# Starting the first weight before the last quarter of x, with two turned columns to a PSUM bank

## The chip, the cores and the metric

The kernel runs on one core of one Trainium2 chip. The metric is the device time of one execution in microseconds, as a median over runs. The engines that matter here are PE (TensorE: matrix products and transposes), ACT (ScalarE), DVE (VectorE), POOL (GpSimd) and SP, whose queue issues the loads.

## What is computed

A trunk of two layers on x (256 tokens x 1024), all in fp32. Each layer is a SwiGLU block, a mixer (windowed attention beside a convolution), a second SwiGLU block and a gated embedding:

```python
for i in range(DEPTH):
    h = x + 0.5 * swiglu(rms_norm(x, norm_ffn1[i]), w_ffn1_in[i], w_ffn1_out[i])
    u = rms_norm(h, norm_mix[i])
    ...
    h = h + (g_attn * y_attn + g_conv * y_conv) @ w_o[i]
    h = h + 0.5 * swiglu(rms_norm(h, norm_ffn2[i]), w_ffn2_in[i], w_ffn2_out[i])
    x = h + (p[i] @ w_pe_proj[i]) * jax.nn.sigmoid(rms_norm(h, norm_pe[i]) @ w_pe_gate[i])
```

Only the very beginning matters here: x is read, turned so that the 1024 features lie on partitions, scaled by the gain norm_ffn1, and multiplied with the first columns of w_ffn1_in. The division by the root mean square is applied after the product, so the squares of x are needed only later.

## The kernel before

**Split numbers.** Every fp32 operand of a product is split in a high part (rounded to fp32r) and a low part (the rest). A product takes three steps for each block of 128 features: high by high, high by low, low by high. A weight is a block of 1024 x 128: 8 feature blocks, so 24 steps of 128x256. ACT makes the high part of a weight (`w_hi`, line 108), DVE the low part (`w_lo`, line 109, source less high part).

**Loading and splitting weights.** `Weights` holds the order of all pieces. SP issues their loads (line 82) into five `raw` buffers, of which x takes one (`x_ld`, line 197, in four quarters of 256 columns). `prep_upto` splits them into seven pairs of buffers. `get` hands out the next weight and splits ahead (`LOOK`, less `rest`); `later` puts a function in front of a later `get`. The first four weights (`quick`) are loaded as pieces of 512 KB for themselves: 0 and 1 make the first pair of products (gate and up), 2 and 3 the second.

**The start.** The order of ACT and DVE at the start is written by hand (`manual_schedule`), and PE's transposes and fillers are kept in program order. In this document column k of x is the block of 128 features number k. For each k PE does fillers (`work`, line 190: products of a constant, whose only use is to keep PE busy), then two transposes (line 517, one for each half of the tokens) into the PSUM tile `xT[k]`. ACT makes the high part `x0h` (line 523) and DVE the low part `x0l` (line 524), both from PSUM. Later `keep_x` copies `xT[k]` to `x32` (line 505; ACT does k = 5 and 7, DVE the others), ACT squares it (lines 443 and 445), and POOL adds the squares (line 446). The squares have two buffers, so ACT's square waits for POOL's add two places back.

PSUM has eight banks of 512 fp32 values per partition: four tiles of one bank (`mm_tile`) and two of two banks (`at_tile`). Before, columns 2 to 5 have an `mm_tile` each; 0 and 6, and 1 and 7, share an `at_tile`, each column in a bank for itself.

After the turning PE does four fillers (`BRIDGE`) and then weight 0 in `by_pass` (line 351): all eight steps of high by high, then x's low part, then the weight's low part. From the second pair on, `mm3` (line 342) does the three steps of one feature block after the other, so it wants the weight's low part at its third step.

Of the kernel before, what the change touches and what calls it, by code (L numbers as in the profile page):

```python
# [9 lines left out]
F32 = mybir.dt.float32  # L10
F32R = mybir.dt.float32r
AF = mybir.ActivationFunctionType
# [3 lines left out]
P = 128  # L16
T = 256
# [19 lines left out]
BACKGROUND = 800  # L37
WEIGHTS_LAG = 100
ATTN = 7
WARM, WAIT, BRIDGE = 7, (0, 0, 1, 0, 2, 0, 2, 0), 4  # L40
W_BUFS = 7
ROW = 64
G0, G1, G2 = 24, 16, 8
# [3 lines left out]
class Weights:  # L47
# [4 lines left out]
    def __init__(self, tc, raw_pool, w_pool):  # L52
        self.tc, self.nc = tc, tc.nc
        self.raw_pool, self.w_pool = raw_pool, w_pool
        self.units, self.specs = [], []
        self.raw, self.ready, self.held, self.hooks = {}, {}, {}, []
        self.next_load = self.next_prep = self.next_get = 0
        self.behind = ()
        self.rest, self.pin, self.lag, self.parts = 0, None, 0, 1

    def unit(self, k, n, sources):
        self.units.append((k, n, sources))
# [13 lines left out]
    def load_upto(self, u):  # L76
        while self.next_load <= min(u, self.limit(), len(self.units) - 1):
            k, n, sources = self.units[self.next_load]
            t = self.raw_pool.tile([P, KD * 256], F32, name="raw", tag="raw")
            v = t[:, : k * n].rearrange("p (k n) -> p k n", n=n)  # L80
            for place, src in sources:
                self.nc.sync.dma_start(place(v), src)
            self.raw[self.next_load] = v
            self.next_load += 1

    def prep_upto(self, i):
        nc = self.nc
        while self.next_prep <= min(i, len(self.specs) - 1):
            k, n, pieces, as_is, place = self.specs[self.next_prep]
            for u, *_ in pieces:  # L90
                self.load_upto(u + RAW_BUFS - 2)
                if u >= self.next_load:
                    return
            if as_is:
                ((u, k0, s0, _, w),) = pieces
                self.ready[self.next_prep] = self.raw[u][:, k0 : k0 + k, s0 : s0 + w]
                self.next_prep += 1
                continue
# [4 lines left out]
            step = k // self.parts  # L103
            for a, (u, k0, s0, d0, w) in ((a, p) for a in range(0, k, step) for p in pieces):
                at = slice(a, a + step)
                src = self.raw[u][:, k0 + a : k0 + a + step, s0 : s0 + w]
                parts = (
                    nc.scalar.copy(out=hv[:, at, d0 : d0 + w], in_=src),  # L108
                    nc.vector.tensor_tensor(  # L109
                        out=lv[:, at, d0 : d0 + w],  # L110
                        in0=src,
                        in1=hv[:, at, d0 : d0 + w].bitcast(F32),
                        op=ALU.subtract,
                    ),
                )
# [40 lines left out]
def encoder_kernel(ctx: ExitStack, tc: tile.TileContext, a: dict, out: bass.AP):  # L156
# [18 lines left out]
    def mm_tile(name):  # L175
        return mmp.tile([P, 512], F32, name=name, tag="mm")
# [18 lines left out]
    for i in range(4):  # L195
# [31 lines left out]


    ws = Weights(tc, raw_pool, w_pool)

    def whole(v):
        return v

    def cols_unit(w, k, c0, n):
        return ws.unit(k, n, [(whole, w[: k * P, c0 : c0 + n].rearrange("(k p) n -> p k n", p=P))])

    def ffn_specs(w_in, w_out, quick=False):
        for j in range(KF // 2):
            if quick and j == 0:
                for c in range(2):  # L240
                    for c0 in (0, FF):
                        u = cols_unit(w_in, KD, c0 + c * P, P)
                        ws.spec(KD, P, [(u, 0, 0, 0, P)])
                continue
            ug = cols_unit(w_in, KD, j * 256, 256)
            uu = cols_unit(w_in, KD, FF + j * 256, 256)
            for c in range(2):
                ws.spec(KD, P, [(ug, 0, c * P, 0, P)])
                ws.spec(KD, P, [(uu, 0, c * P, 0, P)])
        for f in range(KD // 2):  # L250
            us = [
                ws.unit(n, 256, [(whole, w_out[k0 * P : (k0 + n) * P, f * 256 : (f + 1) * 256].rearrange("(k p) n -> p k n", p=P))])
                for k0, n in KGROUPS
            ]
            for c in range(2):
                for u, (_, n) in zip(us, KGROUPS):
                    ws.spec(n, P, [(u, 0, c * P, 0, P)])
# [85 lines left out]
                if pin:  # L343
                    tc.keep_in_program_order(mm)

    def by_pass(ps, w, x):

        (wh, wl), (xh, xl) = w, x
        for i, (wa, xa) in enumerate(((wh, xh), (wh, xl), (wl, xh))):
            for k in range(KD):  # L350
                nc.tensor.matmul(
                    ps, wa[:, k, :], xa[:, k, :], start=i == 0 and k == 0, stop=i == 2 and k == KD - 1
                )

    def pair(name, x, fresh, early=False):


        if early and fresh:
            ps = mm_tile(name)
            work(BRIDGE, ps)  # L360
            ps = ps.rearrange("p (c t) -> p c t", c=2)
            return ps, [lambda c=c: by_pass(ps[:, c, :], ws.get(), x) for c in range(2)]
        if not fresh:
            ps = mm_tile(name).rearrange("p (c t) -> p c t", c=2)
            return ps, [lambda c=c: mm3(ps[:, c, :], ws.get(), x) for c in range(2)]
# [12 lines left out]
        return ps, [lambda: start(0), end]  # L378
# [116 lines left out]


    x_first = x_cur = new_x("xa", "x0")
    stat = Stat()
    with tc.manual_schedule(engines={mybir.EngineType.Activation, mybir.EngineType.DVE}):
        n_par = place_params(rows_first, ("norm_ffn1",), 0, mm_tile)  # L500
        xT = {}

        def keep_x(k):
            copy = nc.scalar.copy if k in (5, 7) else nc.vector.tensor_copy
            copy(out=x32[:, k, :], in_=xT[k])


        shared = [at_tile("ps_xt") for _ in range(2)]
        for k in range(KD):
            if 2 <= k < 6:  # L510
                xT[k] = mm_tile("ps_xt")[:, :T]
            else:
                c0 = 0 if k < 2 else 512
                xT[k] = shared[k % 2][:, c0 : c0 + T]
            work(WAIT[k], xT[k])
            for t in range(2):
                turned = nc.tensor.transpose(
                    xT[k][:, t * P : (t + 1) * P], x_ld[:, t, k * P : (k + 1) * P], ident
                )
                tc.keep_in_program_order(turned)  # L520
            gain = pcol("norm_ffn1", 0, k)
            xh, xl = (x[:, k, :] for x in x_cur)
            nc.scalar.activation(out=xh, in_=xT[k], func=AF.Copy, scale=gain)
            nc.vector.scalar_tensor_tensor(
                out=xl, in0=xT[k], scalar=gain, in1=xh.bitcast(F32), op0=ALU.mult, op1=ALU.subtract
            )
# [742 lines left out]
```

## Time and profile before

| what | us |
|---|---|
| median of three runs | 1090.41 (1089.34 to 1090.47) |
| the profiled execution | 1088.88 |
| its span on the core | 1087.1 |
| PE's first step on weight 0 | 9.66 |
| PE's first step on weight 1 | 12.61 |
| PE's first step on weight 2 | 15.33 |
| SP's issues of x and the first nine pieces | 0.72 to 19.4 |

A row of the timeline has the start in us from the span's start, the duration from the first start to the last end, the engine, the line in the kernel before, the operation, the tile written and those read, and how many instructions it stands for; in brackets is how long the engine had been idle ahead of it, and what it waited for. Instructions overlap at their ends, so a row of two is shorter than twice one. A row of the groups has the line, engine, operation, shapes and count, then busy us and mean ns of one, then idle us ahead of them and what ended most of it. A row of waits has who waited for whom, the total in us, how often, and the longest.

### The profile page before, as it was taken

What the parts mean: (1) busy time and instruction counts of PE and PEld (TensorE: products, weight loads), DVE (VectorE), ACT (ScalarE), POOL (GpSimd) and SP (SyncE); (2) the same over time, 40 slices, a digit from 0 to 9 for tenths busy, and PEclk for the clock granted to TensorE, in tenths of its full rate; (3) what the DMA queues carried; (4) which work ended last, traced back from release to release, by engine and by line L of the source; (5) the groups of instructions that cost most, each with busy time, mean ns of one, the idle gap of its engine ahead of it and who ended that gap; (6) DMA issues with size and microseconds to landing.
All of it is one profiled execution on the core that took longest, in us unless ns stands there. A gap on an engine that the chain in (4) does not pass through costs nothing.

```text
span 1087.1 us, 22045 instructions
## 1 busy us (share of the span) xinstructions
PE 1079.0 (99%) x9182; PEld 1059.3 (97%) x9182; DVE 820.7 (75%) x1229; ACT 619.8 (57%) x1039; POOL 84.7 (8%) x123
## 2 busy tenths in 40 slices
PE   9999999999999999999999999999999999999998
PEld 8999999999899999999999999999998999999998
DVE  6877666799989777666887776659999987776664
ACT  7655445676767455445765554447776665554453
POOL 2000001220002000001110000113100100000110
PEclk9999999999999999999999999999999999999999
DMA  9876546556066646546556554576633666564531
GB/s 311 287 245 221 180 164 225 174 178 179 20 232 226 223 165 219 182 165 230 185 183 209 180 198 148 198 233 194 155 117 131 219 204 210 179 198 148 198 117 39
DMA packets 195439, 203.01 MB, mean 187 GB/s; under 512 B 3731, under 2 KB 188643, under 8 KB 195340
## 3 DMA queue, kind: packets, MB, share of 16 engines
q1 hardware_dynamic: 195308, 201.60, 56.2%
q8 instruction: 72, 1.18, 0.4%
q14 instruction: 27, 0.22, 0.1%
q10 hardware_dynamic: 32, 0.01, 0.0%
HBM read 200.53 MB, written 1.06 MB: 185 GB/s over the span
## 4 chain that ended last, share of the span: by engine, by line
PE 90%; DVE 5%; ACT 2%; issue 1%; DMA 1%; SPq 0%; POOL 0%; POOLq 0%
PE ps_gu L342 43%; PE ps_fo L342 22%; PE ps_c L342 4%; PE ps_wo L342 4%; PE ps_pe L342 4%; PE ps_ao L949 3%; PE ps_g L342 2%; DVE y L672 2%; PE ps_co L1053 2%; DVE w_lo L109 2%; PE ps_pp L342 1%; DVE s L838 1%; ACT s L846 1%; PE ps_q L780 1%; PE ps_q L782 1%
## 5 line engine op out<-in xcount | busy, mean ns | idle before, releaser
L109 DVE TENSOR_TENSOR w_lo<-raw,w_hi 128x1024 fp32r<-128x1024 f32 (+2 forms) x377 | 450.3, 1200 | 198.6 <-ACT w_hi L108 198.5
L108 ACT CAST w_hi<-raw 128x1024 fp32r<-128x1024 f32 (+2 forms) x377 | 387.8, 1035 | 361.2 <-PE ps_gu L342 191.6
L342 PE MATMUL ps_fo<-h_hi,w_lo 128*128 128x256 f32 x704 | 193.0, 275 | 0.0
L342 PE MATMUL ps_fo<-h_lo,w_hi 128*128 128x256 f32 x704 | 193.0, 275 | 0.0
L342 PE MATMUL ps_fo<-h_hi,w_hi 128*128 128x256 f32 x704 | 193.0, 275 | 0.0
L342 PEld LDWEIGHTS ps_fo<-h_lo,w_hi 128*128 128x128 f32 x704 | 131.8, 188 | 0.0
L342 PEld LDWEIGHTS ps_fo<-h_hi,w_hi 128*128 128x128 f32 x704 | 131.8, 188 | 0.0
L342 PEld LDWEIGHTS ps_fo<-h_hi,w_lo 128*128 128x128 f32 x704 | 131.8, 188 | 0.0
L446 POOL TENSOR_TENSOR sq_acc<-sq_acc,sq 128x256 f32<-128x256 f32 x56 | 52.6, 938 | 827.7 <-ACT sq L445 827.4
L672 DVE SCALAR_TENSOR_TENSOR y<-cpad,cw,y 128x256 f32<-128x256 f32 x240 | 100.9, 471 | 0.1
L342 PE MATMUL ps_gu<-xf1l,w_hi 128*128 128x256 f32 x352 | 97.1, 276 | 0.0
L342 PE MATMUL ps_gu<-xf0l,w_hi 128*128 128x256 f32 x352 | 97.1, 276 | 0.0
L342 PE MATMUL ps_gu<-xn0h,w_hi 128*128 128x256 f32 x352 | 97.0, 276 | 0.0
L342 PE MATMUL ps_gu<-xf1h,w_hi 128*128 128x256 f32 x352 | 97.0, 275 | 0.0
L342 PE MATMUL ps_gu<-xf0h,w_hi 128*128 128x256 f32 x352 | 97.0, 275 | 0.0
L342 PE MATMUL ps_gu<-xf0h,w_lo 128*128 128x256 f32 x352 | 96.9, 275 | 0.0
L342 PE MATMUL ps_gu<-xf1h,w_lo 128*128 128x256 f32 x352 | 96.9, 275 | 0.0
L342 PE MATMUL ps_gu<-xn0h,w_lo 128*128 128x256 f32 x352 | 96.8, 275 | 0.0
L342 PE MATMUL ps_gu<-xn0l,w_hi 128*128 128x256 f32 x352 | 96.8, 275 | 0.0
L342 PE MATMUL ps_gu<-x0h,w_lo 128*128 128x256 f32 x336 | 92.8, 276 | 0.3 <-DVE w_lo L109 0.3
L342 PE MATMUL ps_gu<-x0h,w_hi 128*128 128x256 f32 x336 | 92.9, 276 | 0.0
L342 PE MATMUL ps_gu<-x0l,w_hi 128*128 128x256 f32 x336 | 92.5, 275 | 0.0
(260 smaller groups left out, 2683.4 us busy)
## 6 DMA issues: line engine op xcount, KB each, us to landing
raw<-in_w_ffn_in_dram SPq DMA_DIRECT2D x86, 1024.0 KB
raw<-in_w_in_dram SPq DMA_DIRECT2D x30, 1024.0 KB
raw<-in_w_ffn_out_dram SPq DMA_DIRECT2D x32, 896.0 KB
raw<-in_w_ffn_out_dram SPq DMA_DIRECT2D x16, 1024.0 KB
raw<-in_w_o_dram SPq DMA_DIRECT2D x8, 1024.0 KB
raw<-in_w_pe_gate_dram SPq DMA_DIRECT2D x8, 1024.0 KB
raw<-in_w_attn_out_dram SPq DMA_DIRECT2D x8, 512.0 KB
raw<-in_w_conv_out_dram SPq DMA_DIRECT2D x4, 1024.0 KB
```

What stands on the lines that cost most here:

```text
L108: nc.scalar.copy(out=hv[:, at, d0 : d0 + w], in_=src),
L109: nc.vector.tensor_tensor(out=lv[:, at, d0 : d0 + w], in0=src, in1=hv[:, at, d0 : d0 + w].bitcast(F32), op=ALU.subtract,),
L342: mm = nc.tensor.matmul(ps, wa[:, k0 + k, cols], xa[:, kx, :], start=a, stop=b)
L446: nc.gpsimd.tensor_tensor(out=self.acc, in0=self.acc, in1=sq, op=ALU.add)
L672: last_tap[0] = nc.vector.scalar_tensor_tensor(out=y[:, i, :], in0=src, scalar=w, in1=y[:, i, :], op0=ALU.mult, op1=ALU.add)
L780: nc.tensor.matmul(o_, u[0][:, kx, ts], wh[:, k, :], start=kx == 0, stop=False)
L782: nc.tensor.matmul(o_, u[1][:, kx, ts], wh[:, k, :], start=False, stop=kx == KD - 1)
L838: nc.vector.tensor_tensor_reduce(out=s[:, c, :], in0=ps[:, c, :], in1=bias[:, v * GROUP + c, off : off + T], scale=1.0, scalar=sink[:, hd ...
L846: nc.scalar.activation(out=s[:, c, :], in_=s[:, c, :], func=AF.Exp, bias=nm[:, c : c + 1], accum_out=den[:, c : c + 1],)
L949: nc.tensor.matmul(ps[:, c * T : (c + 1) * T], w[:, k, c * P : (c + 1) * P], x[:, k, :], start=k == 0, stop=k == KC - 1,)
L1053: mm = nc.tensor.matmul(ps[:, c, :], wa[:, k, c * P : (c + 1) * P], ya[:, k, :], start=(i, k) == (0, 0), stop=(i, k) == (2, KC - 1),)
```

## The change

1. The first piece of weights is loaded in two transfers, feature blocks 0 to 5 (`CUT` = 6) ahead of x's last quarter and blocks 6 and 7 behind it; the second piece in two halves. Their splits are cut at the same places.
2. PE turns columns 0 to 5, then does the high by high steps of weight 0 on blocks 0 to 5 (`by_pass` with an order and with `last=False`), and only then turns columns 6 and 7. The remaining 18 steps follow: low by high and high by low on 0 to 5, then all three on 6 and 7. The first pair's products have a two-bank tile (`first_ps`).
3. The eight turned columns lie in four one-bank tiles, columns 2i and 2i + 1 in the two halves of tile i.
4. All copies to `x32` come after the splits of weights 0 and 1, in order of k. The splits of weights 2 and 3 stand ahead of the squares number 2 and 4 (counted from 0; 2 and 5 before). `get` is called once ahead of the rest, so weights 4 and on are queued one `get` later than before, and the product of the squares' sum (`ps_stat`) too.
5. One warm-up filler fewer (`WARM` 6), and other fillers between the columns.

```diff
-WARM, WAIT, BRIDGE = 7, (0, 0, 1, 0, 2, 0, 2, 0), 4
+WARM, WAIT, BRIDGE = 6, (0, 0, 2, 0, 1, 0, 0, 0), 4
+CUT = 6
...
             for i, (place, src) in enumerate(sources):
                 self.nc.sync.dma_start(place(v), src)
+                if (self.next_load, i) == (0, 0):
+                    self.between()
...
+    for i in range(3):
+        load_x(i)
...
+    ws.between = lambda: load_x(3)
...
-                        u = cols_unit(w_in, KD, c0 + c * P, P)
+                        u = cols_unit(w_in, KD, c0 + c * P, P, (() if c else (KC,) if c0 else (CUT,)))
...
         if early and fresh:
-            ps = mm_tile(name)
-            work(BRIDGE, ps)
-            ps = ps.rearrange("p (c t) -> p c t", c=2)
-            return ps, [lambda c=c: by_pass(ps[:, c, :], ws.get(), x) for c in range(2)]
+            order = [(i, 0, KD) for i in range(3)]
+            return first_ps, [lambda: None, lambda: by_pass(first_ps[:, 1, :], ws.get(), x, order)]
...
+    first_ps = at_tile("ps_gu").rearrange("p (c t) -> p c t", c=2)[:, :, :T]
...
-        shared = [at_tile("ps_xt") for _ in range(2)]
-        for k in range(KD):
-            if 2 <= k < 6:
-                xT[k] = mm_tile("ps_xt")[:, :T]
-            else:
-                c0 = 0 if k < 2 else 512
-                xT[k] = shared[k % 2][:, c0 : c0 + T]
+        banks = [mm_tile("ps_xt") for _ in range(KD // 2)]
+
+        def turn_x(k):
+            xT[k] = banks[k // 2][:, k % 2 * T : (k % 2 + 1) * T]
             work(WAIT[k], xT[k])
...
-            if k == 3:
-                keep_x(2)
-                keep_x(3)
-        ws.parts = 2
-        ws.prep_upto(0)
-        ws.parts = 1
+        for k in range(CUT):
+            turn_x(k)
+            first_part(k)
+            second_part(k)
+        splits = []
+        ws.cuts = (CUT,)
+        ws.prep_upto(0, splits)
+        w_first = ws.ready[0]
+        work(BRIDGE, first_ps[:, 0, :])
+        high, low, high_end, low_end = splits
+        high()
+        low()
+        by_pass(first_ps[:, 0, :], w_first, x_cur, ((0, 0, CUT),), last=False)
+        high_end()
+        for k in range(CUT, KD):
+            turn_x(k)
+            first_part(k)
+            second_part(k)
+        low_end()
+        order = ((1, 0, CUT), (2, 0, CUT), (0, CUT, KD), (1, CUT, KD), (2, CUT, KD))
+        by_pass(first_ps[:, 0, :], w_first, x_cur, order, first=False)
+        ws.cuts = (KC,)
         ws.prep_upto(1)
-        for k in (4, 5, 6, 7, 0, 1):
+        ws.cuts = ()
+        order = range(KD)
+        for k in order:
             keep_x(k)
-        for i, k in enumerate((2, 3, 5, 4, 6, 7, 0, 1)):
-            if i in (2, 5):
-                ws.prep_upto(2 + i // 5)
+        for i, k in enumerate(order):
+            if i in (2, 4):
+                ws.prep_upto(1 + i // 2)
             squared = stat.add(x32[:, k, :])
+    ws.rest = LOOK
+    ws.get()
+    ws.rest = 0
```

Where instructions move, the built programs are shown as they stand, an engine's rows in order, with the semaphores that an instruction waits for in brackets: `DMAHW` counts transfers, and the others count the finished instructions of the engine they name.

PE from the first transposes to weight 0, in the program before (line 517 turns a column, line 190 is a filler, line 351 a step):

```order
L517 MATMUL ps_xt<-ident,x_ld 128x128 [waits DMAHW1_49]
L517 MATMUL ps_xt<-ident,x_ld 128x128 x3
L190 MATMUL ps_xt<-ones_d 128x128
L517 MATMUL ps_xt<-ident,x_ld 128x128 [waits DMAHW2_49]
L517 MATMUL ps_xt<-ident,x_ld 128x128 x3
L190 MATMUL ps_xt<-ones_d 128x128 [waits PE_49]
L190 MATMUL ps_xt<-ones_d 128x128
L517 MATMUL ps_xt<-ident,x_ld 128x128 [waits DMAHW3_49]
```

And in the program after, in the same place (lines 530, 195 and 367):

```order
L530 MATMUL ps_xt<-ident,x_ld 128x128 [waits DMAHW1_49]
L530 MATMUL ps_xt<-ident,x_ld 128x128
L530 MATMUL ps_xt<-ident,x_ld 128x128 [waits DVE_49]
L530 MATMUL ps_xt<-ident,x_ld 128x128
L195 MATMUL ps_xt<-ones_d 128x128 x2
L530 MATMUL ps_xt<-ident,x_ld 128x128 [waits DMAHW2_49]
...
L367 MATMUL ps_gu<-x0h,w_hi 128x256 [waits Activation_49]
L367 MATMUL ps_gu<-x0h,w_hi 128x256 x5
L530 MATMUL ps_xt<-ident,x_ld 128x128 [waits DMAHW5_49]
L530 MATMUL ps_xt<-ident,x_ld 128x128
L530 MATMUL ps_xt<-ident,x_ld 128x128 [waits DVE_49]
L530 MATMUL ps_xt<-ident,x_ld 128x128
```

Two columns followed each other on PE with no wait between them; now the second column of each bank stands behind a wait on DVE, and the last bank's two columns stand between the first six steps of weight 0 and the others.

ACT from the split of weight 1 to that of weight 3, in the program before (line 108 casts a weight, 505 copies a column, 443 and 445 square):

```order
L108 CAST w_hi<-raw 128x1024 [waits DMAHW6_49]
L505 COPY x_117<-ps_xt 128x256 [waits DVE_49] x2
L443 ACTIVATE sq_acc<-x_117 128x256
L445 ACTIVATE sq<-x_117 128x256
L108 CAST w_hi<-raw 128x1024 [waits DMAHW7_49]
L445 ACTIVATE sq<-x_117 128x256 [waits Activation_49]
L445 ACTIVATE sq<-x_117 128x256 [waits DVE_49,Pool_49] x2
L108 CAST w_hi<-raw 128x1024 [waits DMAHW0_49]
```

And in the program after (lines 112, 521, 458 and 460):

```order
L112 CAST w_hi<-raw 128x512 [waits DMAHW7_49]
L112 CAST w_hi<-raw 128x512 [waits DMAHW0_49]
L521 COPY x_115<-ps_xt 128x256 [waits DVE_49] x2
L458 ACTIVATE sq_acc<-x_115 128x256
L460 ACTIVATE sq<-x_115 128x256
L112 CAST w_hi<-raw 128x1024 [waits DMAHW1_49]
L460 ACTIVATE sq<-x_115 128x256
L460 ACTIVATE sq<-x_115 128x256 [waits Pool_49]
L112 CAST w_hi<-raw 128x1024 [waits DMAHW2_49]
```

Both programs have the two copies ahead of the cast of weight 2. Before, they waited for the low parts of columns 5 and 7 on DVE; now the columns share banks with 4 and 6, and the copies wait for DVE's copies of those, which stand fifth and sixth in DVE's row:

```order
L539 SCALAR_TENSOR_TENSOR x0l<-ps_xt,par,x0h 128x256 [waits Activation_49] x6
L113 TENSOR_TENSOR w_lo<-raw,w_hi 128x768 [waits DMAHW4_49,Activation_49]
L539 SCALAR_TENSOR_TENSOR x0l<-ps_xt,par,x0h 128x256 [waits Activation_49] x2
L113 TENSOR_TENSOR w_lo<-raw,w_hi 128x256 [waits DMAHW6_49]
L113 TENSOR_TENSOR w_lo<-raw,w_hi 128x512 [waits DMAHW7_49,Activation_49]
L113 TENSOR_TENSOR w_lo<-raw,w_hi 128x512 [waits DMAHW0_49,Activation_49]
L521 COPY x_115<-ps_xt 128x256 x6
L113 TENSOR_TENSOR w_lo<-raw,w_hi 128x1024 [waits DMAHW1_49,Activation_49]
```

DVE did two of its copies among the low parts of x and four ahead of weight 2's low part; now all six stand ahead of that.

More of the change, by code (lines that the diff above doesn't have):

```diff
@@ L58, in __init__ @@
         self.behind = ()
-        self.rest, self.pin, self.lag, self.parts = 0, None, 0, 1
+        self.rest, self.pin, self.lag, self.cuts = 0, None, 0, ()
     def unit(self, k, n, sources):
@@ L80, in load_upto, with prep_upto @@
             v = t[:, : k * n].rearrange("p (k n) -> p k n", n=n)
-            for place, src in sources:
+            for i, (place, src) in enumerate(sources):
                 self.nc.sync.dma_start(place(v), src)
+                if (self.next_load, i) == (0, 0):
+                    self.between()
             self.raw[self.next_load] = v
             self.next_load += 1
-    def prep_upto(self, i):
+    def prep_upto(self, i, calls=None):
         nc = self.nc
@@ L102, in prep_upto @@
             lv = lo[:, place : place + k * n].rearrange("p (k n) -> p k n", n=n)
[L103 to L113, printed above, removed]
-                    ),
-                )
+            ends = (0, *self.cuts, k)
+            for (a, b), (u, k0, s0, d0, w) in ((ab, p) for ab in zip(ends, ends[1:]) for p in pieces):
+                hs, ls = hv[:, a:b, d0 : d0 + w], lv[:, a:b, d0 : d0 + w]
+                src = self.raw[u][:, k0 + a : k0 + b, s0 : s0 + w]
+                made = (
+                    lambda hs=hs, src=src: nc.scalar.copy(out=hs, in_=src),
+                    lambda hs=hs, ls=ls, src=src: nc.vector.tensor_tensor(
+                        out=ls, in0=src, in1=hs.bitcast(F32), op=ALU.subtract
+                    ),
+                )
+                if calls is not None:
+                    calls.extend(made)
+                    continue
+                parts = [call() for call in made]
                 if self.pin:
@@ L194, in encoder_kernel, with load_x @@
     xv = a["x"][0].rearrange("(t p) d -> p t d", p=P)
-    for i in range(4):
+    def load_x(i):
         s = slice(i * 256, (i + 1) * 256)
         nc.sync.dma_start(x_ld[:, :, s], xv[:, :, s])
+    for i in range(3):
+        load_x(i)
     col = {}
@@ L229, in encoder_kernel, with cols_unit @@
     ws = Weights(tc, raw_pool, w_pool)
+    ws.between = lambda: load_x(3)
     def whole(v):
         return v
-    def cols_unit(w, k, c0, n):
-        return ws.unit(k, n, [(whole, w[: k * P, c0 : c0 + n].rearrange("(k p) n -> p k n", p=P))])
+    def cols_unit(w, k, c0, n, cuts=()):
+        src = w[: k * P, c0 : c0 + n].rearrange("(k p) n -> p k n", p=P)
+        ends = (0, *cuts, k)
+        return ws.unit(k, n, [
+            (whole if not cuts else lambda v, a=a, b=b: v[:, a:b], src[:, a:b]) for a, b in zip(ends, ends[1:])
+        ])
     def ffn_specs(w_in, w_out, quick=False):
@@ L344, in mm3, with by_pass @@
                     tc.keep_in_program_order(mm)
-    def by_pass(ps, w, x):
+    def by_pass(ps, w, x, order, first=True, last=True):
         (wh, wl), (xh, xl) = w, x
-        for i, (wa, xa) in enumerate(((wh, xh), (wh, xl), (wl, xh))):
-            for k in range(KD):
-                nc.tensor.matmul(
-                    ps, wa[:, k, :], xa[:, k, :], start=i == 0 and k == 0, stop=i == 2 and k == KD - 1
-                )
+        passes = ((wh, xh), (wh, xl), (wl, xh))
+        steps = [(i, k) for i, k0, k1 in order for k in range(k0, k1)]
+        for n, (i, k) in enumerate(steps):
+            wa, xa = passes[i]
+            mm = nc.tensor.matmul(
+                ps, wa[:, k, :], xa[:, k, :], start=first and n == 0, stop=last and n == len(steps) - 1
+            )
+            tc.keep_in_program_order(mm)
     def pair(name, x, fresh, early=False):
         if early and fresh:
-            ps = mm_tile(name)
-            work(BRIDGE, ps)
-            ps = ps.rearrange("p (c t) -> p c t", c=2)
-            return ps, [lambda c=c: by_pass(ps[:, c, :], ws.get(), x) for c in range(2)]
+            order = [(i, 0, KD) for i in range(3)]
+            return first_ps, [lambda: None, lambda: by_pass(first_ps[:, 1, :], ws.get(), x, order)]
         if not fresh:
@@ L505, in keep_x @@
             copy(out=x32[:, k, :], in_=xT[k])
-        shared = [at_tile("ps_xt") for _ in range(2)]
-        for k in range(KD):
-            if 2 <= k < 6:
-                xT[k] = mm_tile("ps_xt")[:, :T]
-            else:
-                c0 = 0 if k < 2 else 512
-                xT[k] = shared[k % 2][:, c0 : c0 + T]
+        banks = [mm_tile("ps_xt") for _ in range(KD // 2)]
+        def turn_x(k):
+            xT[k] = banks[k // 2][:, k % 2 * T : (k % 2 + 1) * T]
             work(WAIT[k], xT[k])
```

9 lines of the change are left out of this document (5 added, 4 removed).

## Prediction

> **What bounds the kernel now.** I read the page first, then the waits of PE (TensorE), then the first 23 us of the timeline engine by engine, since the diff touches nothing later.
>
> The page's first part gives busy time, share of the span and instructions; the rows of PE's waits give the total, the number and the longest, in us.
>
> ```profile
> span 1087.1 us, 22045 instructions
> PE 1079.0 (99%) x9182; PEld 1059.3 (97%) x9182; DVE 820.7 (75%) x1229; ACT 619.8 (57%) x1039; POOL 84.7 (8%) x123
> ...
> PE ps_pt L865 <- ACT s L857: 1.5, 2, 0.7
> ...
> PE ps_gu L351 <- ACT w_hi L108: 0.6, 1, 0.6
> PE ps_gu L342 <- DVE w_lo L109: 0.3, 1, 0.3
> PE ps_xt L517 <- DMA x_ld<-in_x_dram: 0.2, 1, 0.2
> ```
>
> PE is busy from its first weight to the end and waits hardly anywhere. So the time is: when PE begins on the first weight, plus its steps, plus its stalls. A microsecond lost or won at the front is kept to the end. The front on PE (start, duration, operation, count; fillers and 128x128 fp32 products show two rows each):
>
> ```profile
> 1.12 3.36 PE L190 MATMUL ps_warm<-ones_d 128*128 128x128 f32 x14 [1.12 <-POOL ones_d L183]
> ...
> 4.62 0.66 PE L517 MATMUL ps_xt<-ident,x_ld 128*128 128x128 f32 x4
> ...
> 5.77 0.61 PE L190 MATMUL ps_xt<-ones_d 128*128 128x128 f32 x4
> 6.22 0.60 PE L517 MATMUL ps_xt<-ident,x_ld 128*128 128x128 f32 x4
> ...
> 7.51 0.66 PE L517 MATMUL ps_xt<-ident,x_ld 128*128 128x128 f32 x4 [0.24 <-DMA x_ld<-in_x_dram]
> ...
> 9.66 1.26 PE L351 MATMUL ps_gu<-x0h,w_hi 128*128 128x256 f32 x8 [0.60 <-ACT w_hi L108]
> ...
> 12.61 1.07 PE L351 MATMUL ps_gu<-x0h,w_hi 128*128 128x256 f32 x8
> 13.52 1.07 PE L351 MATMUL ps_gu<-x0l,w_hi 128*128 128x256 f32 x8
> ...
> 15.33 0.28 PE L342 MATMUL ps_gu<-x0h,w_hi 128*128 128x256 f32 x1
> ...
> 15.56 0.28 PE L342 MATMUL ps_gu<-x0h,w_lo 128*128 128x256 f32 x1
> ...
> 18.16 0.28 PE L342 MATMUL ps_gu<-x0l,w_hi 128*128 128x256 f32 x1
> 18.70 0.39 PE L342 MATMUL ps_gu<-x0h,w_lo 128*128 128x256 f32 x1 [0.26 <-DVE w_lo L109]
> ...
> 22.03 0.37 PE L342 MATMUL ps_gu<-x0h,w_lo 128*128 128x256 f32 x1
> ```
>
> PE begins at 9.66 when ACT's cast of the first weight is done, ends that weight at 12.61, the second at 15.33, and stalls at 18.70 for the low half of weight 3. Eight steps take 13.52 - 12.61 = 0.91, so 0.114 each. Beside it ACT, DVE and POOL:
>
> ```profile
> 5.16 0.47 ACT L523 ACTIVATE x0h<-ps_xt,par 128x256 fp32r<-128x256 f32 x1 [0.27 <-PE ps_xt L517]
> 5.53 0.83 ACT L523 ACTIVATE x0h<-ps_xt,par 128x256 fp32r<-128x256 f32 x2
> 5.67 0.48 DVE L524 SCALAR_TENSOR_TENSOR x0l<-ps_xt,par,x0h 128x256 fp32r<-128x256 f32 x1 [5.67 <-ACT x0h L523]
> 7.98 0.47 ACT L523 ACTIVATE x0h<-ps_xt,par 128x256 fp32r<-128x256 f32 x1 [0.51 <-PE ps_xt L517]
> 8.98 1.14 ACT L108 CAST w_hi<-raw 128x512 fp32r<-128x512 f32 x2 [0.17 <-DMA raw<-in_w_ffn_in_dram]
> 9.64 1.29 DVE L109 TENSOR_TENSOR w_lo<-raw,w_hi 128x512 fp32r<-128x512 f32 x2
> 11.50 0.64 ACT L505 COPY x<-ps_xt 128x256 f32<-128x256 f32 x2
> 12.77 1.41 DVE L505 COPY x<-ps_xt 128x256 f32<-128x256 f32 x4
> 13.60 0.73 ACT L445 ACTIVATE sq<-x 128x256 f32<-128x256 f32 x2
> 17.34 1.30 DVE L109 TENSOR_TENSOR w_lo<-raw,w_hi 128x1024 fp32r<-128x1024 f32 x1 [2.02 <-ACT w_hi L108]
> L108 ACT CAST w_hi<-raw 128x1024 fp32r<-128x1024 f32 x12 | 11.9, 1048 | 0.4 <-DMA raw<-in_w_ffn_in_dram 0.4
> L108 ACT CAST w_hi<-raw 128x512 fp32r<-128x512 f32 x2 | 1.1, 616 | 0.2 <-DMA raw<-in_w_ffn_in_dram 0.2
> L446 POOL TENSOR_TENSOR sq_acc<-sq_acc,sq 128x256 f32<-128x256 f32 x7 | 6.9, 991 | 12.1 <-ACT sq L445 11.8
> L109 DVE TENSOR_TENSOR w_lo<-raw,w_hi 128x1024 fp32r<-128x1024 f32 x10 | 11.9, 1224 | 4.7 <-ACT w_hi L108 4.7
> ```
>
> The turned columns go through a pipeline: ACT starts on column 1 at 5.53, before DVE starts on column 0 at 5.67. That overlap is possible because each column has its own tile.
>
> **The shared banks (the largest term).** In the changed program columns 2i and 2i+1 lie in one bank, and the order with its waits shows what follows: the second column's transposes wait on DVE, whose first work of all is column 0's low half. So PE turns column 1 only after ACT and DVE have read column 0. The link, from the rows: transposes to ACT 0.47 (7.51 to 7.98), ACT to DVE 0.51 (5.16 to 5.67), DVE 0.48, and 0.06 back to PE (17.34 + 1.30 to 18.70): 1.52 us between two columns that stood 0.23 apart. Two transposes take 0.23 (half of 6.22 less 5.77), and so does one filler.
>
> The first column starts at 4.4: its landing isn't shown, but it is at or before 4.62, and one warm-up filler fewer frees 0.48 (two rows of 3.36 / 14), so the bounds are 4.1 and 4.6. Then, column by column: 0 at 4.4, 1 at 5.92, two transposes and two fillers, 2 at 6.61, 3 at 8.13, two transposes and one filler, 4 at 8.59, 5 at 10.11. ACT starts on column 5 at 10.58 and is free 0.37 later (5.53 less 5.16), at 10.95. The cast of 6/8 of the first weight (128x768, no row) lies between 0.62 and 1.05; I take 0.83. PE begins at 11.84 with 0.06 for the signal. Before: 9.66. **Term 1: +2.2.**
>
> The early transfer, which is what the change is about, gains nothing here: x's quarters and 3/4 of the piece have landed long before 10.95 (the whole 512 KB piece had at 8.98), and even x's last quarter comes before its turn.
>
> **The first weight.** PE runs six steps (0.68), at 12.52 turns column 6, and column 7 stands next in its queue: it waits until 14.04, and the eighteen other steps of this weight, which need neither, wait behind it. They end at 14.04 + 0.23 + 18 x 0.114 = 16.32; the weight took 9.66 to 12.61, 2.95, and now 4.48. **Term 2: +1.5** (0.45 are the four transposes, which lay ahead of the weight before).
>
> **Weight 2's low half.** The second weight ends at 16.32 + 2.72 = 19.04; PE wants weight 2's low half at 19.27. DVE has, from column 7's low half at 14.04 + 0.98 = 15.02: that (0.39 step), the 128x256 rest (about 0.35, under half of the 128x512), two halves of 512 (1.29), at 17.0 six copies where four stood, 0.35 each by 1.41 / 4: the fifth and sixth end at 18.8 and 19.1. ACT's copies of columns 5 and 7 now share banks with these, and wait for them; ACT's queue holds behind them two squares and cast 2. So: copy 7 from 19.1 (0.32), two squares (0.73) to 20.1, cast 1.05 to 21.2, low half 1.22 to 22.45, PE at 22.5. Before: 15.56, with no wait. **Term 3: 22.5 - 19.27 = +3.2.** Check: 22.5 - 15.56 = 6.9 = 2.2 + 1.5 + 3.2.
>
> **Weights 3 and 4.** Weight 3's cast now follows two squares instead of standing behind a third that waits for POOL; its low half is ready near 24, and PE wants it at 25.2. The stall of before goes: 18.16 + 0.114 = 18.27 to 18.70. **Term 4: -0.4.** Weight 4's cast stands behind all squares, as before, and POOL's adds (0.99 each) pace them: the last square starts when five adds after 20.1 are through, 25.2 to 26.6 by mean pace or by the pace of before. So its low half lands at 27.8 to 29.2, wanted at 22.5 + 48 x 0.114 = 28.0. The step of before at 22.03 had the statistics product (0.25) ahead of it, which moves 24 steps later. **Term 5: +0.2, from -0.3 to +0.9.**
>
> The rest is cover: two more issues on SP, cuts of w1 in halves, ten casts ahead of the square root instead of seven (ACT is 1.05 per cast against 2.72 per weight of PE, so it runs ahead), one more DVE and ACT instruction. They cost nothing while weights are ready seven deep; if evacuations came late, PE would wait for a bank at the fifth pair, about 11 us after weight 4 starts, and the root is done about 10 us after cast 4 starts, which itself starts 2.3 us ahead. That is close, so up to +0.5 goes into the range.
>
> Sum: 2.2 + 1.5 + 3.2 - 0.4 + 0.2 = **+6.7 us**. The profiled execution took 1088.88 (span 1087.1 and 1.8 around it); it becomes 1095.6. The median of the three runs shown, 1090.41, lies 1.5 above that execution, so the median I predict is **1097.1**.
>
> **Where the skill speaks.** Row: ACT's 5.53 and DVE's 5.67 overlap, in two tiles. The Trainium skill, PSUM — Partial Sum Buffer, section "PSUM bank collisions raise a hardware error", says that two engines may not be in one bank (on the same partitions) at once, at any address, and that the compiler orders them. By that rule the turning is serial as above, +6.7; by the row alone, it would be the third rival's +0.3. The order's waits side with the rule; no trace here has a shared bank.
>
> **Rivals.**
> 1. *The array falls back to half rate.* The first fillers ran at 3.36 / 14 = 0.24 a row, later ones at about 0.11 (0.45 for four): PE starts slow and becomes fast with use. Between 4.4 and 11.8 it now works only 12 transposes and 7 fillers, 1.4 + 1.6 = 3.0 us of 7.4, and waits 3.2 later. Half rate through the turning adds some 0.1 per transpose pair and 0.23 per filler on the path, and 0.7 in the first six steps: +1.5; half rate in weight 2 adds 24 x 0.1 = 2.4. Against: no single idle stretch is over 2 us up to the first weight. Time: 1097.1 + 1.5 to 2.4, so 1098.6 to 1099.5. Chance 0.14. The Trainium skill, TensorE: Matmul & The Clock Gate, Part 1, has the fall need an idle window of about 3.4 us; by that rule this rival would not happen, and no run here shows such a gap.
> 2. *Only the turning is serial; ACT's copies don't hold the squares.* Then cast 2 starts after two squares that follow the second DVE copy (17.7), about 18.5, DVE is free at 19.1, and the low half is there at 20.35: term 3 becomes 1.1, the sum +4.6, the time 1095.0. Against: the order shows the wait on both copies. Chance 0.07.
> 3. *Not slower: the waits are met before PE arrives* and the turning overlaps as before. PE then starts when 3/4 of the piece has landed: x's end at 7.51 plus 128 KB more, at the 512 KB per 1.5 us from 7.5 to 8.98, is 7.9; with the cast 8.8. That is -0.9, the four transposes +0.45, DVE's two further copies and the squares ahead of cast 2 make weight 2 late by some 1.2 (its low half near T + 7.35 = 16.15 against 15.56 before), the stall -0.4, weight 4 +0.1: +0.3, 1090.7. It decides at one place: whether column 1's transposes start 0.2 or 1.5 us after column 0's. Against: no filler fills 1.3 us there. Chance 0.06. Even with weight 2's wait gone this gives -0.9, so faster by more than 0.2% (2.2 us) would need PE to begin at 7.5, before its operand.
>
> **Numbers.** Forecast 0.73, rivals 0.14, 0.07 and 0.06. The forecast's own range comes from the start of column 0 (0.4), the 768 cast (0.2 either way), term 5 (-0.5 to +0.7), late evacuations (0.5) and the spread of the three runs (1089.34 to 1090.47): 1095.4 to 1098.8. With most of rival 1 and the edge of rival 2 the range is 1094.8 to 1099.6. A difference of 0.2%, 2.2 us, is about what a measurement of this kernel can tell from no change; only rival 3 stays within it: same 0.06, faster 0.01, slower 0.93.
>
> **What would show it.** Right: in the timeline, second transposes of each bank 1.5 us behind the first, with PE waiting for DVE x0l; PE's first product of x0h and w_hi near 11.8; a wait of about 1.3 inside the first weight; a wait of 3 us for w_hi and w_lo of weight 2; from weight 6 on the same steps as before, some 6.7 us later, and no other stage changed. Wrong: first product before 10.5, or ACT's two copies running before DVE's, or fillers and steps at 0.2 us after 11 us.

## The result, and the profile after

The changed kernel takes 1099.48 us (median of five runs, 1099.31 to 1100.87), the kernel before beside it 1090.01 (1089.34 to 1090.47): a ratio of 1.0089, interval 1.0075 to 1.0103, so 9.5 us slower. The forecast was 1097.1, with a range of its own from 1095.4 to 1098.8. The sign and the place were right; 2.4 us were missing, and the time lies above that range, where the prediction's first rival had it.

The profiled execution of the kernel after took 1100.87 (span 1099.1). Its PE timeline at the front, in the columns of the rows of before:

```profile
4.26 0.69 PE L530 MATMUL ps_xt<-ident,x_ld 128*128 128x128 f32 x2
6.10 0.69 PE L530 MATMUL ps_xt<-ident,x_ld 128*128 128x128 f32 x2 [1.15 <-DVE x0l L539]
...
7.43 0.63 PE L530 MATMUL ps_xt<-ident,x_ld 128*128 128x128 f32 x2
9.15 0.69 PE L530 MATMUL ps_xt<-ident,x_ld 128*128 128x128 f32 x2 [1.08 <-DVE x0l L539]
...
12.26 1.91 PE L195 MATMUL ps_gu<-ones_d 128*128 128x128 f32 x8
13.83 1.63 PE L367 MATMUL ps_gu<-x0h,w_hi 128*128 128x256 f32 x6
...
16.97 0.69 PE L530 MATMUL ps_xt<-ident,x_ld 128*128 128x128 f32 x2 [1.08 <-DVE x0l L539]
17.31 1.63 PE L367 MATMUL ps_gu<-x0l,w_hi 128*128 128x256 f32 x6
...
20.80 1.10 PE L367 MATMUL ps_gu<-x0h,w_hi 128*128 128x256 f32 x8
...
24.23 0.39 PE L356 MATMUL ps_gu<-x0h,w_hi 128*128 128x256 f32 x1 [0.53 <-ACT w_hi L112]
...
25.49 0.39 PE L356 MATMUL ps_gu<-x0h,w_lo 128*128 128x256 f32 x1 [0.76 <-DVE w_lo L113]
```

Two things are to be seen. The second column of a bank starts 1.84 and 1.72 behind the first, each time after a wait for DVE's low part: the serial turning that was forecast. And PE is slow whenever it works: six steps from 17.31 take 1.42 to the next row (18.73), 0.236 each, where eight at 20.80 take 0.93, 0.116 each. The eight rows of four fillers take 1.57 (12.26 to 13.83), 0.20 a row; in the kernel before, fillers took 0.11 a row in the turning. This slowness, called half rate below, lasts to about 20.

PE's waits show the four links; before, there was no row of `x0l`:

```profile
PE ps_xt L530 <- DVE x0l L539: 4.4, 4, 1.2
...
PE ps_gu L356 <- DVE w_lo L113: 1.6, 2, 0.8
```

Ahead of weight 2 the row of DVE and ACT is as forecast: six copies, ACT's two copies behind them, two squares, the cast, the low half.

```profile
20.14 2.07 DVE L521 COPY x<-ps_xt 128x256 f32<-128x256 f32 x6
21.92 0.71 ACT L521 COPY x<-ps_xt 128x256 f32<-128x256 f32 x2 [2.72 <-DVE x L521]
...
23.14 1.04 ACT L112 CAST w_hi<-raw 128x1024 fp32r<-128x1024 f32 x1
24.21 1.23 DVE L113 TENSOR_TENSOR w_lo<-raw,w_hi 128x1024 fp32r<-128x1024 f32 x1 [2.00 <-ACT w_hi L112]
```

Past the front nothing is lost to the change. PE's first `ps_c` step (a product for the mixer's convolution, behind the first SwiGLU block) stands at these places, before and after:

```profile
192.20 0.28 PE L342 MATMUL ps_c<-xm0h,w_hi 128*128 128x256 f32 x1
202.88 0.28 PE L356 MATMUL ps_c<-xm0h,w_hi 128*128 128x256 f32 x1
```

It comes 10.7 later. The profiled pair ends 12.0 apart; of the other 1.3, 1.1 lies in the attention stages, where this execution waits 2.6 for `s` and the one of before 1.5. Executions below wait there 1.5 to 2.1 with any front, so I count none of it.

### The profile page after: what moved, and what is told of

It reads as the page before. It is cut to its first block, busy times and chain, and to the rows that moved or that the text cites. A ratio compares the mean times of both kernels' runs of the same rounds, so it can differ in the third digit from the quotient of the medians.

```text
span 1099.1 us, 22033 instructions
## 1 busy us (share of the span) xinstructions
PE 1084.7 (99%) x9176; PEld 1063.0 (97%) x9176; DVE 821.9 (75%) x1230; ACT 620.6 (56%) x1040; POOL 86.1 (8%) x123
## 4 chain that ended last, share of the span: by engine, by line
PE 82%; DVE 9%; ACT 4%; POOL 2%; issue 2%; POOLq 0%; ACTq 0%
PE ps_gu L356 43%; PE ps_fo L356 22%; PE ps_wo L356 4%; PE ps_pe L356 4%; DVE y L710 3%; DVE w_lo L113 3%; PE ps_ao L987 3%; PE ps_co L1091 2%; ACT w_hi L112 1%; PE ps_c L356 1%; PE ps_pp L356 1%; POOL ms L756 1%; DVE s L876 1%; PE ps_g L356 1%; ACT s L884 1%
```

## The experiments

Theory A: neighbours in one bank make the turning and the copies serial, and that is all (6.7). Theory B: besides, the gaps so made hold PE at half rate, which the forecast had as a rival. Rival C: it is the cut first weight, the transposes inside it and the new orders. Differences are between medians, to the kernel before on the same chip (1088.92, 1089.65, 1089.38 and 1089.57 in the four groups of runs); `ps_c` stands for the start of PE's first `ps_c` step (192.20 before).

**Sharing alone, in the kernel before.**

```diff
-        shared = [at_tile("ps_xt") for _ in range(2)]
+        banks = [mm_tile("ps_xt") for _ in range(KD // 2)]
...
+            xT[k] = banks[k // 2][:, k % 2 * T : (k % 2 + 1) * T]
```

(The first pair's products move to a two-bank tile, to make room.)

> The kernel before, with nothing changed but that columns 2i and 2i + 1 share a bank. Theory A: four links of 1.5 to 1.7 in place of 0.23, PE's first step on weight 0 near 14 in place of 9.66, and the wait for weight 2's low half under 1 since the order of the squares and copies is before's: 4 to 5 above before at full rate, 1094 to 1095. With theory B too: half rate through weight 0, 2 to 3 more, 1096 to 1098. If sharing alone costs little (rival C): under 1092.

Measured: 1097.02, ratio 1.0070 (1.0056 to 1.0083), 8.1 above before; `ps_c` at 200.77. PE's timeline of this run:

```profile
12.14 0.69 PE L513 MATMUL ps_xt<-ident,x_ld 128*128 128x128 f32 x2 [1.08 <-DVE x0l L520]
...
15.68 1.92 PE L190 MATMUL ps_gu<-ones_d 128*128 128x128 f32 x8
17.24 2.05 PE L351 MATMUL ps_gu<-x0h,w_hi 128*128 128x256 f32 x8
...
21.81 1.07 PE L351 MATMUL ps_gu<-x0h,w_hi 128*128 128x256 f32 x8
```

Sharing alone makes most of the loss, and here too rows are slow, to about 21: fillers, then eight steps in 1.85 (17.24 to 19.09). PE starts weight 0 at 17.24, 3 later than theory A says at full rate. This program has the seven warm-up fillers of before, so PE stays slow without the change's one filler fewer too. Rival C falls as the main cause.

**The kernel after without shared neighbours.**

```diff
-            xT[k] = banks[k // 2][:, k % 2 * T : (k % 2 + 1) * T]
+            xT[k] = banks[k % 4][:, k // 4 * T : (k // 4 + 1) * T]
```

> The kernel after, with columns k and k + 4 in one bank in place of 2i and 2i + 1. Theory A (the sharing by neighbours makes the turning serial, and with it ACT's and DVE's copies) and theory B (the gaps so made keep PE at half rate until 20 us) both say: no wait of PE for x0l, steps of 0.114 from the first on, PE's first step on weight 0 near 8.8, weight 2's third step near 16.2, the whole about 0.3 above before, 1090.3, from 1089.3 to 1091.5. Rival C (the cut first weight, the transposes inside it and the order of DVE's copies cost most of it): PE begins early, but the whole stays over 1094.

Measured: 1091.8, ratio 1.0026 (1.0016 to 1.0036), 2.9 above before; `ps_c` at 195.09. Its PE timeline, and its stretches with PE's busy time and, third from the end, the granted clock:

```profile
8.38 0.97 PE L367 MATMUL ps_gu<-x0h,w_hi 128*128 128x256 f32 x6 [0.54 <-ACT w_hi L112]
...
13.54 1.07 PE L367 MATMUL ps_gu<-x0h,w_lo 128*128 128x256 f32 x8
15.87 0.38 PE L356 MATMUL ps_gu<-x0h,w_hi 128*128 128x256 f32 x1 [1.26 <-ACT w_hi L112]
...
17.13 0.38 PE L356 MATMUL ps_gu<-x0h,w_lo 128*128 128x256 f32 x1 [0.76 <-DVE w_lo L113]
```

```profile
16.00:18.00 2.00, 1.24 (x8) 1.04 (x9) 1.67 (x2) 1.67 (x4) 1.64 (x2) 0.93 1.08 382
18.00:20.00 2.00, 2.00 (x11) 2.00 (x11) 0.75 (x1) 0.54 (x2) 1.92 (x2) 0.50 1.08 379
```

ACT's two copies in it:

```profile
13.23 0.37 ACT L521 COPY x<-ps_xt 128x256 f32<-128x256 f32 x1 [1.75 <-DVE x L521]
13.89 0.37 ACT L521 COPY x<-ps_xt 128x256 f32<-128x256 f32 x1 [0.29 <-DVE x L521]
```

The wait for `x0l` is gone and PE starts 1.3 earlier than in the kernel before. So 6.6 of the 9.5 go with the shared neighbours; the 2.9 that are left belong to the rest of the change. (Sharing alone cost 8.1 in the kernel before: the two parts don't simply add up.) The columns still share banks, 5 with 1 and 7 with 3, and ACT's copies of 5 and 7 still wait for DVE's copies of 1 and 3, 1.75 and 0.29, as the two rows show. So a part of the 2.9 is probably sharing too; no run has the change without any sharing. Weight 2's third step comes at 17.13 (forecast for this case: about 16.15), since its cast stands behind these two copies and two squares on ACT, and its low half behind six copies on DVE. Then something unforeseen follows: from 17.7 to 20.9 steps take 0.213, and the granted clock reads 0.50. From the end of weight 1 (14.45) to 17.13 PE had done only two steps.

**That wait, filled.** Eleven fillers ahead of weight 2, and nothing else:

```diff
+            if x is x_first and not filled:
+                filled.append(work(11, ps))
```

> The kernel with columns k and k + 4 in one bank, and eleven fillers on PE ahead of weight 2, as long as the wait that the run without them has there (14.45 to 17.13). The fillers take nothing away from that wait: weight 2's third step stays at 17.1 to 17.3. If the steps at 0.213 from 17.7 to 20.9 in that run were the cost of PE's idle time, they go: all steps at 0.114, the first step of weight 4 about 1.5 earlier, and the whole 1.3 to 1.5 above before in place of 2.9. If half rate there has another cause: 2.9 above before, as without the fillers.

Measured: 1091.3, ratio 1.0017 (1.0008 to 1.0026), 1.65 above before; `ps_c` at 194.10, 1.0 earlier.

```profile
14.58 2.62 PE L195 MATMUL ps_gu<-ones_d 128*128 128x128 f32 x22
16.96 0.36 PE L356 MATMUL ps_gu<-x0h,w_hi 128*128 128x256 f32 x1
...
17.28 0.34 PE L356 MATMUL ps_gu<-x0h,w_lo 128*128 128x256 f32 x1
...
20.11 0.28 PE L356 MATMUL ps_gu<-x0h,w_lo 128*128 128x256 f32 x1
...
23.90 0.39 PE L356 MATMUL ps_gu<-x0h,w_lo 128*128 128x256 f32 x1 [0.39 <-DVE w_lo L113]
```

The product that was late is no earlier (17.28 against 17.13), yet all steps behind it take 0.114, and later work comes 1.0 earlier. So half rate is the price of thin work, apart from the wait that made it thin. The times alone would not settle it (the intervals overlap); the rows do.

**The shared banks kept, PE kept at work.** First five fillers after each even column, into a PSUM tile of their own (`gap_ps`), with one warm-up filler more:

```diff
+            if k % 2 == 0:
+                work(5, gap_ps)
```

> The kernel after, its shared banks kept, with five fillers after each even column and one warm-up filler more, in a tile of their own, so that PE works through the waits. Theory B says: steps and fillers run at 0.114 from 5 us on, the four links come back to 1.5 from 1.7, PE begins weight 0 near 12.3, weight 2's third step comes near 23, and the whole is 2 to 3.5 below after: 1096 to 1097.5. If half rate has another cause than thin work, or costs nothing: rows of 0.2 to 0.24 each as in after, and the whole at 1099.5 or, with 20 slow fillers on the path, above.

Measured: 1097.25, ratio 1.0078 (1.0065 to 1.0091), 8.3 above before; `ps_c` at 200.62. The first link is 1.93, with fillers at half rate still; from the second on the links are 1.46 to 1.47, and PE starts weight 0 at 12.36, as expected. But half rate comes back further on, where the row of fillers ends:

```profile
21.65 0.39 PE L356 MATMUL ps_gu<-x0h,w_hi 128*128 128x256 f32 x1 [1.75 <-ACT w_hi L112]
...
22.91 0.58 PE L356 MATMUL ps_gu<-x0h,w_lo 128*128 128x256 f32 x1 [0.76 <-DVE w_lo L113]
23.29 0.42 PE L356 MATMUL ps_gu<-x0h,w_hi 128*128 128x256 f32 x1
```

So I filled that wait as well, with eleven fillers ahead of weight 2 as above:

> The kernel after with fillers through the turning (five after each even column, one warm-up filler more) and eleven more ahead of weight 2: its shared banks and every wait kept, but PE at work all along. If the forecast's chain of waits was right and only half rate was left out, PE runs at full rate to the end of weight 2, weight 2's third step comes at 22.9 to 23.2, and the whole is 6.7 to 7.2 above before (the forecast's sum was 6.7). If half rate was no cost of its own: 8.3 above before, as with the first fillers alone.

Measured: 1096.79, ratio 1.0067 (1.0055 to 1.0080), **7.1 above before**; `ps_c` at 199.44, 7.2 later.

```profile
4.57 0.44 PE L537 MATMUL ps_xt<-ident,x_ld 128*128 128x128 f32 x2
...
6.16 0.44 PE L537 MATMUL ps_xt<-ident,x_ld 128*128 128x128 f32 x2
...
12.03 0.98 PE L367 MATMUL ps_gu<-x0h,w_hi 128*128 128x256 f32 x6 [0.39 <-ACT w_hi L112]
...
16.64 1.07 PE L367 MATMUL ps_gu<-x0h,w_hi 128*128 128x256 f32 x8
...
22.58 0.39 PE L356 MATMUL ps_gu<-x0h,w_lo 128*128 128x256 f32 x1 [0.35 <-DVE w_lo L113]
```

Every wait of the change is still in this kernel, and no row after the warm-up is slow. (Up to weight 2 this is the program of the run before, which came to full rate a little later; so the step from 12.36 to 12.03 is not the new fillers' doing.) It is what the forecast's sum describes, and it costs what that sum says, 6.7, within half a microsecond. Theory A alone gives this; A and B give the kernel after.

**The kernel after, once more, and with x's last quarter ahead of all weights.**

```diff
-    for i in range(3):
+    for i in range(4):
         load_x(i)
...
-    ws.between = lambda: load_x(3)
+    ws.between = lambda: None
```

> The kernel after, unchanged, beside the one with x's last quarter ahead of the weights. The links of 1.7, the rows at half rate and the whole at 9.5 above before again. If the time at which PE's rows change from half to full rate isn't set by the program (16.8 in the run of after with the other order, 20.0 in the profile of after, where the first 17 us of both are alike), this profile may show it at another place, and the sum of the front moves by up to 1.5 with it.

> The kernel after, but x's last quarter is issued ahead of all weights. The forecast said that the early transfer gains nothing while the turning is serial, since everything has landed before ACT comes to the first cast: the same as after within 0.5, apart from the 1.5 by which after's own runs differ, and PE's first step on weight 0 at 13.8 as in after. If the early transfer gains there what it gained with columns k and k + 4 in a bank: 0.8 to 1.3 above after.

Measured: after again 1098.83, ratio 1.0089 (1.0076 to 1.0102), 9.45 above before; with the late quarter 1099.41, ratio 1.0091 (1.0078 to 1.0104). No difference, and PE's first step on weight 0 is at 13.76 with the late quarter, so the early transfer gains nothing while the turning is serial, as forecast. The profile of after again, rows and stretches:

```profile
4.20 0.50 PE L530 MATMUL ps_xt<-ident,x_ld 128*128 128x128 f32 x2
...
6.13 0.61 PE L195 MATMUL ps_xt<-ones_d 128*128 128x128 f32 x4
...
8.04 0.69 PE L530 MATMUL ps_xt<-ident,x_ld 128*128 128x128 f32 x2 [1.09 <-DVE x0l L539]
...
12.72 1.63 PE L367 MATMUL ps_gu<-x0h,w_hi 128*128 128x256 f32 x6
...
16.05 0.95 PE L367 MATMUL ps_gu<-x0l,w_hi 128*128 128x256 f32 x6
...
22.86 0.38 PE L356 MATMUL ps_gu<-x0h,w_hi 128*128 128x256 f32 x1 [1.75 <-ACT w_hi L112]
```

```profile
8.00:12.00 4.00, 2.87 (x12) 2.47 (x13) 1.06 (x3) 1.55 (x4) 0.00 (x0) 0.50 1.10 329
12.00:16.00 4.00, 2.92 (x14) 2.52 (x14) 1.83 (x3) 1.37 (x3) 0.00 (x0) 0.67 0.03 8
...
26.00:28.00 2.00, 2.00 (x12) 2.00 (x11) 0.00 (x0) 0.85 (x3) 1.79 (x3) 0.50 1.08 367
```

The same program, and half rate lies elsewhere: fast fillers at 6.13, slow rows from 8.04 to about 14.7 (a mean clock of 0.67 over 12 to 16 makes 1.3 of these 4 us at full rate), fast through the rest of weight 0 (from 16.05) and through weight 1, then 2.9 of waits at weight 2 (1.2 more than in the first profile, since PE came to it earlier), and slow again from 24.9 to 28.2. Either way `ps_c` comes 9.7 to 10.7 late.

**The early transfer where the turning is not serial.** The same edit in the kernel without shared neighbours:

> As the run with columns k and k + 4 in one bank, but x's last quarter is issued ahead of the weights, as in the kernel before. If the early transfer is worth what its bytes take (256 KB, at 512 KB per 1.5 us from 7.5 to 8.98 in the profile of before): PE's first step 0.7 later, and the whole 0.7 above the run with it. If the wait for weight 2's low half swallows an early start: first step 0.7 later, weight 2's third step at the same place, the whole the same within 0.3.

Measured: 1093.07, ratio 1.0035 (1.0022 to 1.0047), 1.3 above the kernel with the early transfer; the intervals overlap, but `ps_c` comes at 195.88, 0.8 later, and PE's first step shows why:

```profile
9.38 0.97 PE L367 MATMUL ps_gu<-x0h,w_hi 128*128 128x256 f32 x6 [1.23 <-ACT w_hi L112]
```

It is 1.0 later than 8.38. The other outcome written down was that the wait at weight 2 swallows this; it did not, for the last two columns, the copies behind them and weight 2's third step (18.13 for 17.13) all come 1.0 later too. So what the change is about is worth about 1 us where the turning is not serial, and its shared neighbours cost 6.6.

**Another order of copies and splits**: ACT's two copies first, weight 2's split behind two of DVE's copies, weight 3's behind two more, the others between squares.

```diff
-        for k in order:
+        for k in (5, 7, 0, 2):
             keep_x(k)
+        ws.prep_upto(2)
+        for k in (4, 6):
+            keep_x(k)
...
-            if i in (2, 4):
-                ws.prep_upto(1 + i // 2)
+            if i in (2, 4, 6):
+                ws.prep_upto(2 + i // 2)
```

In the kernel after, with its shared banks:

> The kernel after, its shared banks kept, with that same order of copies and splits. The profile of after has 1.7 of wait at weight 2 and 0.8 at weight 4 left to take away: 2 to 2.5 below after, 7 to 7.5 above before, 1096 to 1096.5. If the forecast's term 3 (3.2) is all to be had: 3.2 below after. If half rate, once PE no longer waits, lasts further into weight 2: under 1.5 below after.

Measured: 1096.26, ratio 1.0062 (1.0048 to 1.0076), 6.6 above before, 2.9 less than after. PE waits for neither half of weight 2, nor for weight 4. The forecast's term 3 (3.2) lies in this, but not alone: the wait at weight 4 went too, and with the wait at weight 2 the half rate that follows it in after again. In the kernel without shared neighbours:

> The kernel with columns k and k + 4 in one bank, and another order on ACT and DVE: ACT's two copies (columns 5 and 7) first, so that they wait for no copy of DVE; the split of weight 2 behind two of DVE's copies, that of weight 3 behind two more, those of 4 and 5 between the squares. If the late low half of weight 2 was what took back the early start, cast 2 runs at 12.1, the low half is there at 14.5, PE waits under 0.3 for it and never falls to half rate: third step of weight 2 at 14.7 (15.56 before), weight 4's at 20.1 to 20.5 (22.03), the whole 1 to 1.7 below before, about 1087.5. If the wait only moves to weight 3 or 4 (their splits, POOL's adds, the loads): within 0.7 of before or above it.

Measured: 1092.41, ratio 1.0027 (1.0016 to 1.0039), 2.8 above before: nothing gained. ACT's copies no longer wait, and the wait at weight 2 is down to 0.2, but others take its place. ACT's timeline and PE's waits:

```profile
18.88 1.04 ACT L112 CAST w_hi<-raw 128x1024 fp32r<-128x1024 f32 x1 [3.24 <-DMA raw<-in_w_ffn_in_dram]
...
22.96 1.05 ACT L112 CAST w_hi<-raw 128x1024 fp32r<-128x1024 f32 x1 [2.40 <-DMA raw<-in_w_ffn_in_dram]
```

```profile
PE ps_stat L471 <- POOL sq_acc L461: 2.1, 1, 2.1
PE ps_gu L356 <- ACT w_hi L112: 1.7, 1, 1.7
```

With this order the later parameters' loads went ahead of weight 4's piece on SP, and the cast of weight 5, waiting for its piece, held the last squares. Two repairs (pieces kept in place on SP, weight 5's split behind the squares):

> The kernel with columns k and k + 4 in one bank and ACT's copies first, with two repairs: the first nine pieces of weights keep their place on SP ahead of the later parameters' loads (in the run before, those loads went ahead, and weight 4's cast waited for its piece until 18.88), and the split of weight 5 stands behind all squares again (there it held the last two up, and PE waited 2.1 for their sum). If those two were all that took the gain back: no wait of PE over 0.4 up to weight 6, third step of weight 4 at 20.2 to 20.6 (22.03 before), 1.0 to 1.6 below before, 1088.0 to 1088.6 against 1089.6. If the loads or POOL's adds bound the front anyway: within 0.6 of before.

Measured: 1091.51, ratio 1.0024 (1.0014 to 1.0035). The front is repaired, PE comes to `ps_par` at 37.76 (38.26 before), and then waits 2.2 at `ps_cw` for a copy of `par` behind ACT's casts. With those tables one pair later:

> The run before with the second order of copies and splits, and the tables made from the later parameters (ps_cw, ps_rb) put one pair of weights later, so that PE comes to them after ACT has copied ps_par. In the run before, PE was 0.5 ahead of before's profile at ps_par (37.76 against 38.26) and then waited 2.24 there and 0.33 at the next. If these two were all that took the rest back: no wait of PE from weight 0 to the attention over 0.4, and the whole 0 to 0.8 below before: 1088.6 to 1089.4 against 1089.4. If something else is late there (ACT's queue behind the cast that waits for its piece until 37.4): the same wait at another tile, and the whole still 1.5 to 2.5 above before.

Measured: 1091.9, ratio 1.0028 (1.0017 to 1.0038). The second theory held: the wait sits at the next tiles.

```profile
PE ps_rb L633 <- ACT cw L622: 1.6, 1, 1.6
```

None of these beats the kernel before. ACT's cast at 37 to 39 waits 5.7 to 5.9 for its piece in both, with ACT's whole queue behind it, where in the kernel before it waits 4.6 until 36.6; why the pieces come later there was not tried.

## Why the prediction came out as it did

"At work all along" is the run with fillers in all gaps, which has one warm-up filler more than the forecast counted on.

| PE, us | before | forecast | at work all along | after | after again |
|---|---|---|---|---|---|
| first step on weight 0 | 9.66 | 11.84 | 12.03 | 13.83 | 12.72 |
| weight 0 takes | 2.95 | 4.48 | 4.61 | 6.97 | 5.51 |
| third step of weight 2 | 15.56 | 22.5 | 22.58 | 25.49 | 24.12 |
| `ps_c`, less before's | 0 | 6.7 | 7.2 | 10.7 | 9.7 |

- **The step that failed** is the weighing of rival 1, "the array falls back to half rate". The forecast's sum takes every filler, transpose and step at full rate, and the rival got a chance of 0.14, with "Against: no single idle stretch is over 2 us up to the first weight". Half rate came in every profile of a kernel with shared neighbours whose gaps weren't filled, with no wait over 1.8, and the sign that the prediction named for it, "fillers and steps at 0.2 us after 11 us", is what the first profile shows. It is worth the difference between the kernel after and the one that is kept at work, each to before, 9.47 - 7.14 = 2.3, near the upper end of the 1.5 to 2.4 that the rival had, and the rival's time (1098.6 to 1099.5) is what was measured. So the weighing was wrong: I asked whether PE would idle long enough to fall, and the rows of before had shown that it first has to be busy long enough to rise (fourteen slow rows, 3.36).
- **That the rival's price fits is in part luck.** It was worked out for half rate in the turning and the first six steps, or in weight 2. In the first profile half rate lay in the turning and in most of weight 0 and cost 4.2 up to weight 1 (20.80 against 16.64 at work all along); a shorter wait at weight 2 took 1.3 of it back (25.49 against 22.58 leaves 2.9). In after again it lay in parts of both.
- **Terms 1 and 2** hold at full rate: 11.84 became 12.03, with column 0 at 4.57 where 4.4 was forecast, behind one warm-up filler more; 4.48 became 4.61. The link of 1.52 is 1.46 to 1.59 there, and 1.72 to 1.84 at half rate.
- **Term 3** is right: weight 2's third step at 22.58 for 22.5. In the first profile of after only 1.7 of it shows (PE could have gone on at 23.78 and did at 25.49), for PE came later to it.
- **Term 4**, the stall for weight 3, went as forecast. **Term 5** was too small, for two reasons. Weight 4's low half came at the late end of the forecast's 27.8 to 29.2 (PE goes on at 29.22 in the run at work, after a wait of 0.38; in the profile of after it waits 0.83, to 32.15). And the term takes off 0.25 because the product of the squares' sum comes 24 steps later; but that product is still done (at 34.80 in after), so nothing is saved by it, and without this slip the sum is about 7.0, beside the 7.1 measured at work all along.
- **Rival 3**, the turning not serial, was built: 2.9 above before instead of 0.3. Of the 2.6 between, 1.0 is weight 2's third step (17.13 for 16.15), where ACT's copies still wait for DVE's, 1.0 to 1.2 half rate again, and 0.3 a wait at weight 4, which the run with fillers shows (0.39).
- "The early transfer gains nothing here" holds in the kernel after.
- "No other stage changed" holds, but for the wait in the attention stages that differs from one execution to another.

## What to carry to other kernels

Before two streams are put in the two halves of a PSUM bank, look who reads the first half when the second is written: here neighbours shared, and a pipeline of three engines became a chain, 6.6 us for eight columns; columns four apart shared without a wait on PE, though ACT's copies still waited 2.0 for DVE's copies out of the same banks. When a change opens gaps on PE, price the rate of the work between the gaps too, not only the gaps. Fillers that do nothing for the result bought 1.0 to 2.3 us here, and an earlier start of PE is worth only what the queues behind it (ACT's casts, SP's loads) can follow.

## What the runs showed of the hardware

- PE's rate. Steps of 0.213 to 0.236 against 0.114. Thin work can keep it low: in the first profile of after it did not rise from 4.26 to about 20, with PE working between waits of 1.1. One stretch of 4.1 without a wait (11.78 to 15.88) did not raise it either. It falls after thin work: two steps in 2.7 us (14.45 to 17.13) were enough; a single wait of 2.1 between dense rows (25.35 to 27.58, in the run with the other order and no shared neighbours) was not. The slow stretches after a fall last 3.2 (17.7 to 20.9), 3.3 (24.9 to 28.2) and some twice that (from between 7.0 and 8.0 to 14.7).
- When it changes isn't set by the program alone: the kernel after changed to full rate at 20.0 in one profile, and near 4.3 and at 14.7 in the other.
- The Trainium skill, TensorE: Matmul & The Clock Gate, Part 1, has the rate follow a free-running window of about 3.4 us: up after a busy one, down after an idle one. The lengths and the wandering start agree. Where it asks for an idle window, the runs differ: stretches with two steps, or with six transposes and two fillers (4.2 to 8.0 in after again), counted as idle.
- The granted clock of the stretches reads 0.50 after a fall, but 1.00 in the first profile of after to 20, where PE had not risen: there only the duration of a step shows it.
